# Normed activations and one feed-forward's gated rows at other byte positions in SBUF, an adaLN ring of two tiles, masks loaded as bytes

## The chip, the cores and the metric

The kernel runs on one core of a Trainium2 chip. The metric is the time of one execution in microseconds of device time; three runs of the kernel before gave 1816.92, 1817.19 and 1819.23 us, so a median of 1817.19 us. One more execution was recorded by the hardware profiler; it took 1819.16 us, and its span, from the first to the last instruction, is 1817.5 us.

## The reference

The model is a two-layer backbone over 256 latent tokens with 256 context tokens as a prefix, 1024 channels wide. Each layer is a feed-forward, a token mixer and a second feed-forward. Each of the three begins with an RMS norm that is scaled and shifted by vectors computed from a condition (adaLN), and its result is added back through a gate vector.

```python
def _swiglu(h, w1, w3, w2):
    return (jax.nn.silu(h @ w1) * (h @ w3)) @ w2
...
ml = _modulation(c, w_ada[l], b_ada[l])          # 9 vectors of 1024: silu(c) @ w_ada + b_ada
lat = lat + 0.5 * ml[2] * _swiglu(_modulate(lat, norm_ffn1_g[l], ml[0], ml[1]), *ffn1)
cx = cx + 0.5 * mc[2] * _swiglu(_modulate(cx, norm_ffn1_g[l], mc[0], mc[1]), *ffn1)
...                                              # token mixer: one input projection, spatial gating,
...                                              # a two-way gated recurrence, one output projection
lat = lat + 0.5 * ml[8] * _swiglu(_modulate(lat, norm_ffn2_g[l], ml[6], ml[7]), *ffn2)
```

The feed-forward is 2816 wide. Context tokens use the same weights; in the last layer only latent tokens go through the output projection and the second feed-forward.

## The kernel before

**Matmuls.** Every large product is made in three matmuls, because each float32 operand is split into a high and a low part (`mm3`, lines 285 to 288): high by high on L286, low activation by high weight on L287, high activation by low weight on L288 (where the weight is the moving operand the names are swapped). The weight block of 128x128 is the stationary operand. The activations are the moving one, in rows of 512 columns where latent and context tokens go together (`BOTH`), and of 256 columns where one of them goes alone (`LAT`, `CTXC`). The token-major units of the mixer (`tm_unit`, the i and v columns) turn this around: 128 tokens of the activations are stationary, and 256 weight columns move.

**Activations in SBUF.** `h_hi` and `h_lo` hold the normed activations: 8 blocks of 512 floats in each partition, one block for each 128 channels, the first 256 floats latent, the rest context. The norm writes them (`modulate`: ACT writes `h_hi`, DVE writes `h_lo`), and the up projections of the feed-forward and the mixer read them. `g_hi` and `g_lo` hold the gated rows of a feed-forward, 22 blocks, which the down projection reads. In the built program `h_hi` begins at byte 34304 of each partition and `h_lo` at 50688; both are multiples of 512. `g_hi` begins at byte 139072, and `g_lo` at 184128 (rows of 512) or at 161600 (the last feed-forward, rows of 256); all three are 320 bytes past a multiple of 512. A block is 2048 bytes (1024 in the last feed-forward's g, and each half of an h block is 1024), so every row of one buffer has its buffer's remainder. The split weights `whi` and `wlo` lie in four slots each, all at 64 bytes past a multiple of 512.

**Weights.** A weight piece is 512 rows by 256 columns (512 KB; some have half the rows). SP issues its DMA into one of 3 raw tiles, ACT copies it to `whi` (L187), DVE subtracts to get `wlo` (L191), and 4 such split pairs exist. A list made by `plan` sets the order of the pieces, and `pump` issues loads and splits ahead as far as the buffers allow.

**adaLN.** The modulation matrices are read in pieces `wada` of 128 x 512 floats (256 KB), 256 of them after the first few. They stand between the weight pieces in the plan, up to two at a time; they lie in a ring of `N_ADA` = 3 tiles. When the plan comes to one, `ada_sum` lets DVE multiply it by the condition and add it to `acc` (L247 for the first of eight, L249 for the others; twice for most pieces, once for the latent and once for the context condition). After eight pieces PE adds up the partitions (`ada_rows`, L258), in its own queue between two weight pieces. `pump` issues the next `wada` loads on SP right after a sum has been written down, each into the tile that was summed longest ago, so it waits for that sum on DVE.

**Masks.** The recurrence uses 7 masks of 128x128 bytes. They are loaded as float32 into `mf` at the start, and POOL casts them to bytes (L1019).

**Order.** Everything is issued in the order of the code; each engine works through its own queue. Around a feed-forward: 11 pairs of up columns (each four weight pieces), then four groups of down columns.

Of the kernel before, what the change touches and what calls it, by code (L numbers as in the profile page):

```python
# [10 lines left out]
F32 = mybir.dt.float32  # L11
F32R = mybir.dt.float32r
# [5 lines left out]
P = 128  # L18
# [3 lines left out]
T = SEQ + CTX  # L22
DEPTH = 2
GRID_W = 64
FF = 2816
KT = D // P
FT = FF // P
# [2 lines left out]
EPS = 1e-6  # L30
POS_THETA = 10000.0
NLEV = 7

COL = {"u": 0, "v": 512, "q": 1024, "f": 1536, "b": 2048, "i": 2560, "g": 3072}
LAT = (0, SEQ)
# [16 lines left out]
def level_masks():  # L52
    x = np.arange(P)[:, None] ^ np.arange(P)[None, :]
    m = np.stack([(x >> lev) == 1 for lev in range(NLEV)], axis=1)
    return np.ascontiguousarray(m.reshape(P, NLEV * P).astype(np.float32))

# [14 lines left out]
class Trunk:  # L73
    N_RAW = 3
    N_SPLIT = 4
    N_ADA = 3

    def __init__(self, tc, es, io):
        self.tc = tc
# [22 lines left out]
    def plan(self):  # L102
# [28 lines left out]
        for l in range(DEPTH):  # L131
            ws += ffn(l, 1, True) + mixer(l) + out(l) + ffn(l, 2, l + 1 < DEPTH)
# [23 lines left out]
    def pump(self):  # L156
        nc = self.nc
        moved = True
        while moved:
            moved = False  # L160
            if self.n_load >= 4 and self.a_load < min(len(self.adas), self.a_done + self.N_ADA):
                it = self.adas[self.a_load]
                _, l, j, half, k = it.key
                c0 = j * D + 512 * half
                it.raw = self.wp.tile([P, 512], F32, tag="ada", name="wada", bufs=self.N_ADA)
                nc.sync.dma_start(it.raw, self.io["w_ada"][l, k * P:(k + 1) * P, c0:c0 + 512])
# [117 lines left out]
    def mm3(self, ps, l_hi, l_lo, r_hi, r_lo, start, stop, swap=False):  # L284
        mm = self.nc.tensor.matmul
        mm(ps, lhsT=l_hi, rhs=r_hi, start=start, stop=False)  # L286
        mm(ps, lhsT=l_hi, rhs=r_lo, start=False, stop=False)  # L287
        mm(ps, lhsT=l_lo, rhs=r_hi, start=False, stop=stop)  # L288
# [113 lines left out]
    def ffn(self, l, n, both):  # L402
        nc = self.nc
        tc = self.tc
        w1, w3, w2 = (f"ffn{n}_w{i}" for i in (1, 3, 2))
        tokens = T if both else SEQ
        j0 = 0 if n == 1 else 6
        whole = BOTH if both else LAT
        with tc.tile_pool(name=f"g{l}{n}", bufs=1) as gp:
            g_hi = gp.tile([P, FT, tokens], F32R, tag="g_hi", name="g_hi")  # L410
            g_lo = gp.tile([P, FT, tokens], F32R, tag="g_lo", name="g_lo")

            silu = {}

            def gate(h, p, span, part):
                for j in range(2):
                    f = 2 * p + j
                    hi, lo = g_hi[:, f, span[0]:span[1]], g_lo[:, f, span[0]:span[1]]
                    ps = h[j][:, :span[1] - span[0]]
                    if part == 1:  # L420
                        silu[j] = self.sp.tile([P, 512], F32, tag="silu", name="silu", bufs=2)[:, :span[1] - span[0]]
                        nc.scalar.activation(silu[j], ps, AF.Silu)  # L422
                    else:
                        nc.vector.tensor_tensor(silu[j], silu[j], ps, op=ALU.mult)  # L424
                        self.split(hi, lo, silu[j])

            def up(p, span, its, keep=False):
                for part, w in ((1, w1), (3, w3)):
                    h = [self.bank(), self.bank()]
                    for i, k0 in enumerate((0, 4)):  # L430
                        it = its[part, k0] if its and not keep else self.take(w, l, k0, 256 * p)
                        self.fm(it, h, self.h_hi, self.h_lo, span, KT)
                        if keep:
                            its[part, k0] = it
                        else:
                            self.done(it)
                    gate(h, p, span, part)

            if self.begun:
                hs = self.begun  # L440
                self.begun = None
                for part, w in ((1, w1), (3, w3)):
                    it = self.take(w, l, 4, 0)
                    self.fm(it, hs[part], self.h_hi, self.h_lo, BOTH, KT)
                    self.done(it)
                    gate(hs[part], 0, whole, part)
            elif both:
                its = {0: None}
                up(0, LAT, its, keep=True)
                self.drain()  # L450
                up(0, CTXC, its)
            else:
                self.drain()
                up(0, LAT, None)
            for p in range(1, FF // 256):
                up(p, whole, None)

            def down(p, span):
                ps = [self.bank(), self.bank()]
                for k0 in range(0, FT, 4):  # L460
                    it = self.take(w2, l, k0, 256 * p)
                    self.fm(it, ps, g_hi, g_lo, span, FT)
                    self.done(it)
                self.update(l, j0 + 2, p, ps, span)

            for p in range(3):
                down(p, whole)
            down(3, LAT)
            if n == 1 or l + 1 < DEPTH:
                nl, nj = (l, 3) if n == 1 else (l + 1, 0)  # L470
                self.behind(self.norm(nl, nj, 0, NF[0]))
                if both:
                    down(3, CTXC)
                    self.drain()
                    self.behind(self.norm(nl, nj, 1, NF[1]))
# [18 lines left out]
    def hgrn(self, l, hp, mp, F, KB, q, V, ready, oT, ended):  # L494
# [12 lines left out]
        def keys(lev):  # L507
            b = 1 << lev
            ka = mp.tile([P, 2, nq], F32, tag="ks", name="ka", bufs=2 * two)
            for d in range(2):  # L510
                nc.scalar.activation(self.halves(ka, b)[d], self.halves(KB[:, d, :, :nq], b)[d], AF.Copy)
            return ka
# [22 lines left out]
        yield HQ[l]  # L535
        for lev in range(NLEV):
            b = 1 << lev
# [3 lines left out]
            for d in range(2):  # L541
                t = F[:, d, :, :n].rearrange("p h (n two) -> p h n two", two=2)
                kh = self.halves(KB[:, d], b)[d]
                tt(kh, kh, t[:, :, :, 1 - d, None].to_broadcast([P, 2, n // 2, b]), op=mult)
            if lev < NLEV - 1:
                ka = keys(lev + 1)
# [84 lines left out]
    def mixer(self, l):  # L631
# [7 lines left out]
        with tc.tile_pool(name=f"mix{l}", bufs=1) as mp:  # L639
# [196 lines left out]
            self.drain()  # L836
            self.behind(self.norm(l, 6, 1, NF[3]))


    def start(self):  # L840
        nc = self.nc
        io = self.io
        cp = self.cp
# [9 lines left out]
        for s in range(2):  # L853
            nc.vector.memset(self.sel[:, s, s:s + 1], 1.0)
        self.x = cp.tile([P, KT, T], F32, tag="x", name="x")
        self.h_hi = cp.tile([P, KT, T], F32R, tag="h_hi", name="h_hi")
        self.h_lo = cp.tile([P, KT, T], F32R, tag="h_lo", name="h_lo")
        self.ssq = cp.tile([P, T], F32, tag="ssq", name="ssq")
        self.mods = cp.tile([P, DEPTH * N_MOD, 2, KT], F32, tag="mods", name="mods")
        self.lb = cp.tile([P, 2, 2, 4], F32, tag="lb", name="lb")  # L860
        self.vec = [cp.tile([P, P], F32, tag=f"vec{l}", name="vec") for l in range(DEPTH)]
        self.masks = cp.tile([P, NLEV, P], U8, tag="masks", name="masks")
        with self.tc.tile_pool(name="start", bufs=1) as st:
            self.table(AF.Silu)
            cc = st.tile([16, P], F32, tag="cc", name="cc")
            pos = st.tile([P, 4 * 4 + 4 * GRID_W], F32, tag="pos", name="pos")
            mf = st.tile([P, NLEV * P], F32, tag="mf", name="mf")
            small = [(pos, io["pos"]), (cc[0:8, :], io["c"].rearrange("o (k p) -> (o k) p", p=P)),
                     (cc[8:16, :], io["c_ctx"].rearrange("(k p) -> k p", p=P))]
            rows = []  # L870
            for l, names in enumerate((("norm_ffn1_g", "norm_mix_g", "norm_ffn2_g", "norm_final_g"),
# [3 lines left out]
                at = 72  # L875
# [5 lines left out]
                    small.append((vr[at:at + r.shape[0], :], r))  # L881
                    at += r.shape[0]
                rows.append((vr, at))
            small.append((mf, io["masks"]))
            xs, raws = {}, {}

            def load(dst, src, after=1):
# [128 lines left out]
                self.fm(it, hs[part], self.h_hi, self.h_lo, BOTH, KT)  # L1016
                self.done(it)
            self.begun = hs
            nc.gpsimd.tensor_copy(self.masks.rearrange("p l t -> p (l t)"), mf)  # L1019

    def final(self):
        nc = self.nc
# [56 lines left out]
```

## Time and profile before

| | |
|---|---|
| median of three runs | 1817.19 us |
| profiled execution, its time | 1819.16 us |
| its span | 1817.5 us |
| mean granted TensorE clock | 0.995 |
| PE busy | 1785.7 us (98%) |
| DVE busy | 1125.8 us (62%) |
| ACT busy | 670.5 us (37%) |
| DMA, mean | 147 GB/s |

PE's busy time counts a matmul until its modelled end, and the next begins before that end. So a PE that is busy all the time can still run at different paces: the pace is the distance between the starts of two matmuls that follow each other, which the timeline gives.

### The profile page before, as it was taken

How to read it: one execution, taken by the hardware profiler on the slowest of the kernel's cores; microseconds unless marked ns; L12 is line 12 of the kernel's file. 1: busy time of each engine (PE TensorE's matmuls, PEld its weight loads, DVE VectorE, ACT ScalarE, POOL GpSimd, SP SyncE). 2: the span in 40 equal slices, each digit the busy share in tenths (PEclk: the TensorE clock that was granted, in tenths of full speed). 3: DMA queues.
4: the chain of work that ended last, by engine and by line, in shares of the span. 5: the costliest groups of instructions: out<-in, count | busy, mean ns of one | idle time of the engine just before them, and what ended most of it. 6: DMA issues, size and time to landing. Idle time of an engine off the chain costs nothing. (4 is left out here: it accounts for less than half of the span.)

```text
span 1817.5 us, 27049 instructions
## 1 busy us (share of the span) xinstructions
PE 1785.7 (98%) x10853; PEld 1547.7 (85%) x10853; DVE 1125.8 (62%) x1746; ACT 670.5 (37%) x1087; POOL 20.6 (1%) x27
## 2 busy tenths in 40 slices
PE   7999999999999999999999999999999999989998
PEld 5777778899898898777788897777788999979998
DVE  4766676675737666666666676545445767665554
ACT  3322222236444343222222242222222555544443
POOL 0000000000000000000000000000000000000000
PEclk9999999999999999999999999999999999989999
DMA  9555555554212124555454544544454532446653
GB/s 327 167 171 157 173 157 164 181 190 126 70 59 82 59 59 146 153 154 156 145 151 153 185 138 147 159 152 149 153 166 140 157 105 86 136 128 186 186 186 117
DMA packets 230645, 266.99 MB, mean 147 GB/s; under 512 B 10368, under 2 KB 192248, under 8 KB 230520
## 3 DMA queue, kind: packets, MB, share of 16 engines
q1 hardware_dynamic: 230520, 265.27, 47.2%
q8 instruction: 85, 1.39, 0.3%
q14 instruction: 40, 0.33, 0.1%
HBM read 264.18 MB, written 1.05 MB: 146 GB/s over the span
## 5 line engine op out<-in xcount | busy, mean ns | idle before, releaser
L286 PE MATMUL mm<-h_hi,whi 128*128 128x512 f32 (+1 forms) x2016 | 712.2, 353 | 4.9 <-ACT h_hi L383 3.0
L287 PE MATMUL mm<-h_lo,whi 128*128 128x512 f32 (+1 forms) x2016 | 705.2, 350 | 1.5 <-DVE h_lo L372 1.0
L288 PE MATMUL mm<-h_hi,wlo 128*128 128x512 f32 (+1 forms) x2016 | 702.6, 349 | 0.0
L191 DVE TENSOR_TENSOR wlo<-wraw,whi 128x1024 fp32r<-128x1024 f32 x362 | 430.7, 1195 | 371.8 <-ACT whi L187 367.8
L187 ACT ACTIVATE whi<-wraw 128x1024 fp32r<-128x1024 f32 x362 | 370.9, 1031 | 409.0 <-PE mm L287 288.0
L286 PEld LDWEIGHTS mm<-h_hi,whi 128*128 128x128 f32 x2016 | 381.0, 189 | 63.0 <-issue 4.0
L287 PEld LDWEIGHTS mm<-h_lo,whi 128*128 128x128 f32 x2016 | 382.7, 190 | 56.7 <-DVE h_lo L372 5.6
L288 PEld LDWEIGHTS mm<-h_hi,wlo 128*128 128x128 f32 x2016 | 380.7, 189 | 53.5
L286 PE MATMUL mm<-g_hi,whi 128*128 128x256 f32 (+1 forms) x836 | 282.1, 337 | 0.0
L288 PE MATMUL mm<-g_hi,wlo 128*128 128x256 f32 (+1 forms) x836 | 278.8, 334 | 0.0
L287 PE MATMUL mm<-g_lo,whi 128*128 128x256 f32 (+1 forms) x836 | 278.8, 333 | 0.0
L249 DVE SCALAR_TENSOR_TENSOR acc<-wada,cond,acc 128x512 f32<-128x512 f32 x392 | 274.0, 746 | 4.3 <-DMA wada<-in_w_ada_dram 3.4
L286 PEld LDWEIGHTS mm<-g_hi,whi 128*128 128x128 f32 x836 | 158.1, 189 | 18.3 <-issue 2.4
L288 PEld LDWEIGHTS mm<-g_hi,wlo 128*128 128x128 f32 x836 | 158.1, 189 | 16.0
L287 PEld LDWEIGHTS mm<-g_lo,whi 128*128 128x128 f32 x836 | 158.2, 189 | 15.2
L187 ACT ACTIVATE g_hi<-silu 128x512 fp32r<-128x512 f32 (+1 forms) x92 | 51.7, 562 | 182.9 <-DVE silu L424 181.0
L422 ACT ACTIVATE silu<-mm 128x512 f32<-128x512 f32 (+1 forms) x92 | 48.3, 528 | 139.7 <-PE mm L288 135.4
L191 DVE TENSOR_TENSOR g_lo<-silu,g_hi 128x512 fp32r<-128x512 f32 (+1 forms) x92 | 55.7, 605 | 57.9 <-ACT g_hi L187 57.9
L424 DVE TENSOR_TENSOR silu<-silu,mm 128x512 f32<-128x512 f32 (+1 forms) x92 | 54.9, 597 | 36.4 <-PE mm L288 36.4
L286 PE MATMUL mm<-whi,h_hi 128*128 128x256 f32 x224 | 64.3, 287 | 0.0
L287 PE MATMUL mm<-wlo,h_hi 128*128 128x256 f32 x224 | 62.6, 279 | 0.0
L288 PE MATMUL mm<-whi,h_lo 128*128 128x256 f32 x224 | 62.5, 279 | 0.0
(129 smaller groups left out, 1053.0 us busy)
## 6 DMA issues: line engine op xcount, KB each, us to landing
wraw<-in_ffn_w_dram SPq DMA_DIRECT2D x271, 512.0 KB, 4.3
wada<-in_w_ada_dram SPq DMA_DIRECT2D x256, 256.0 KB, 3.2
wraw<-in_w_in_dram SPq DMA_DIRECT2D x56, 512.0 KB, 3.6
a<-in_w_ada_dram SPq DMA_DIRECT2D x8, 1024.0 KB, 9.6
wraw<-in_w_out_dram SPq DMA_DIRECT2D x16, 512.0 KB, 3.9
wraw<-in_ffn_w_dram SPq DMA_DIRECT2D x19, 256.0 KB
x<-in_x_dram SPq DMA_DIRECT2D x2, 512.0 KB
ctx<-in_ctx_dram SPq DMA_DIRECT2D x2, 512.0 KB, 5.8
```

Of the source, the lines that this page charges most:

```text
L187: self.nc.scalar.activation(hi, src, AF.Copy)
L191: self.nc.vector.tensor_tensor(lo, src, hi.bitcast(F32), op=ALU.subtract)
L249: nc.vector.scalar_tensor_tensor(acc[:, s], raw, c, acc[:, s], op0=ALU.mult, op1=ALU.add)
L286: mm(ps, lhsT=l_hi, rhs=r_hi, start=start, stop=False)
L287: mm(ps, lhsT=l_hi, rhs=r_lo, start=False, stop=False)
L288: mm(ps, lhsT=l_lo, rhs=r_hi, start=False, stop=stop)
L422: nc.scalar.activation(silu[j], ps, AF.Silu)
L424: nc.vector.tensor_tensor(silu[j], silu[j], ps, op=ALU.mult)
```

## The change

Four things change.

1. `h_hi` and `h_lo` become longer buffers, `h_all`, and the rows have two homes in them, 80 floats (320 bytes) apart. `home(80)` is taken at the start: `h_hi` then begins at byte 34624 and `h_lo` at 52032, both 320 bytes past a multiple of 512. After the up projections of the last layer's first feed-forward, `home(0)` is taken: 34304 and 51712, both multiples of 512. From there on the last layer's mixer and its last feed-forward use it.
2. `g_hi` gets 128 or 48 unused floats ahead of it. With rows of 512 the gated rows lie where they lay (139072 and 184128). In the last feed-forward they lie at 138752 and 161280, both multiples of 512.
3. `N_ADA` goes from 3 to 2.
4. The masks are made as bytes and loaded straight into their place; `mf` and the cast go.

In the built program the split weights move by 1536 bytes, so they are still 64 bytes past a multiple of 512, and every other tile keeps its remainder by 512.

```diff
-    return np.ascontiguousarray(m.reshape(P, NLEV * P).astype(np.float32))
+    return np.ascontiguousarray(m.reshape(P, NLEV * P).astype(np.uint8))
...
-    N_ADA = 3
+    N_ADA = 2
...
-            g_hi = gp.tile([P, FT, tokens], F32R, tag="g_hi", name="g_hi")
+            lead = 128 if both else 48
+            g_hi = gp.tile([P, lead + FT * tokens], F32R, tag="g_hi", name="g_hi")[:, lead:]
+            g_hi = g_hi.rearrange("p (f t) -> p f t", t=tokens)
             g_lo = gp.tile([P, FT, tokens], F32R, tag="g_lo", name="g_lo")
...
                 up(p, whole, None)
+
+            if (l, n) == (DEPTH - 1, 1):
+                self.home(0)
...
+    def home(self, at):
+        self.h_hi, self.h_lo = (h[:, at:at + KT * T].rearrange("p (k t) -> p k t", t=T) for h in self.h_all)
...
-        self.h_hi = cp.tile([P, KT, T], F32R, tag="h_hi", name="h_hi")
-        self.h_lo = cp.tile([P, KT, T], F32R, tag="h_lo", name="h_lo")
+        self.h_all = [cp.tile([P, KT * T + n], F32R, tag=f"h_{w}", name=f"h_{w}")
+                      for w, n in (("hi", 256), ("lo", 128))]
+        self.home(SHIFT)
...
-            small.append((mf, io["masks"]))
+            small.append((self.masks.rearrange("p l t -> p (l t)"), io["masks"]))
...
-            nc.gpsimd.tensor_copy(self.masks.rearrange("p l t -> p (l t)"), mf)
```

The queues of PE, DVE and ACT hold the same instructions in the same order as before. SP's and POOL's differ in a few rows. SP's queue before, at the end of the start-up loads (`a` are the first adaLN pieces, `wraw` weight pieces):

```order
L891 DMA mf<-in_masks_dram 128x896
L174 DMA wraw<-in_ffn_w_dram 128x4x256 x2
L166 DMA wada<-in_w_ada_dram 128x512 x3
L174 DMA wraw<-in_ffn_w_dram 128x4x256 x5
L166 DMA wada<-in_w_ada_dram 128x512 x2
```

The same place now:

```order
L900 DMA masks<-in_masks_dram 128x896
L175 DMA wraw<-in_ffn_w_dram 128x4x256 x2
L167 DMA wada<-in_w_ada_dram 128x512 x2
L175 DMA wraw<-in_ffn_w_dram 128x4x256 x5
L167 DMA wada<-in_w_ada_dram 128x512 x2
```

Two pieces instead of three are loaded ahead, and each later `wada` load comes one piece later in the plan than it did; the last one moves behind one more weight piece.

POOL's queue before, around the cast (`r` is the reciprocal root of a norm):

```order
masks.py:199 AFFINE_SELECT ident<-ident 128x128
L331 TENSOR_TENSOR r<-ms,mhalf 128x2 x2
L1019 CAST masks<-mf 128x896
L331 TENSOR_TENSOR r<-ms,mhalf 128x2 x2
L331 TENSOR_TENSOR r<-ms,mhalf 128x4 x2
```

And now:

```order
masks.py:199 AFFINE_SELECT ident<-ident 128x128
L332 TENSOR_TENSOR r<-ms,mhalf 128x2 x4
L332 TENSOR_TENSOR r<-ms,mhalf 128x4 x2
L332 TENSOR_TENSOR r<-ms,mhalf 128x16
L332 TENSOR_TENSOR r<-ms,mhalf 128x4 x2
```

The cast is gone from POOL, and the rest stands as it stood.

## Rows read from the trace of the kernel before

**Rows 1.** The page's busy times: us, share of the span, instructions.
```profile
span 1817.5 us, 27049 instructions
PE 1785.7 (98%) x10853; PEld 1547.7 (85%) x10853; DVE 1125.8 (62%) x1746; ACT 670.5 (37%) x1087; POOL 20.6 (1%) x27
```

**Rows 2.** Windows: length; PE, PEld, DVE, ACT, POOL busy (instructions), PEclk, DMA share, GB/s.
```profile
556.30:654.70 98.40, 96.98 (x546) 83.58 (x545) 64.75 (x108) 41.12 (x77) 4.92 (x3) 1.00 0.21 65
702.80:932.00 229.20, 229.20 (x1064) 182.58 (x1064) 143.71 (x197) 66.17 (x87) 0.00 (x0) 1.00 0.52 156
932.00:1024.80 92.80, 92.80 (x449) 75.40 (x448) 58.01 (x85) 21.14 (x26) 0.00 (x0) 1.00 0.52 159
```

**Rows 3.** Groups of instructions, shapes kept apart: count | busy us, mean ns | idle before.
```profile
L286 PE MATMUL mm<-h_hi,whi 128*128 128x512 f32 x1184 | 475.6, 402 | 1.9 <-ACT h_hi L383 1.9
L286 PE MATMUL mm<-h_hi,whi 128*128 128x256 f32 x832 | 236.6, 284 | 3.0 <-ACT h_hi L187 1.9 <-ACT h_hi L383 1.1
L286 PE MATMUL mm<-g_hi,whi 128*128 128x512 f32 x396 | 156.2, 394 | 0.0
L286 PE MATMUL mm<-g_hi,whi 128*128 128x256 f32 x440 | 125.9, 286 | 0.0
```

**Rows 4.** PE's timeline (start, us, what), first and last of 119 512-column matmuls on h.
```profile
737.57 0.40 PE L287 MATMUL mm<-h_lo,whi 128*128 128x512 f32 x1
...
765.10 0.39 PE L288 MATMUL mm<-h_hi,wlo 128*128 128x512 f32 x1
```

**Rows 5.** The same, first and last of 107 512-column matmuls on g.
```profile
975.20 0.39 PE L287 MATMUL mm<-g_lo,whi 128*128 128x512 f32 x1
...
999.26 0.39 PE L288 MATMUL mm<-g_hi,wlo 128*128 128x512 f32 x1
```

**Rows 6.** The same, first and last of 143 256-column matmuls on g.
```profile
386.44 0.28 PE L287 MATMUL mm<-g_lo,whi 128*128 128x256 f32 x1
...
403.48 0.28 PE L288 MATMUL mm<-g_hi,wlo 128*128 128x256 f32 x1
```

**Rows 7.** First and last of 1038 256-column matmuls on h, last feed-forward.
```profile
1622.38 0.28 PE L286 MATMUL mm<-h_hi,whi 128*128 128x256 f32 x1
...
1744.51 0.28 PE L288 MATMUL mm<-h_hi,wlo 128*128 128x256 f32 x1
```

**Rows 8.** First and last of 108 256-column matmuls on h, output projection.
```profile
654.72 0.28 PE L286 MATMUL mm<-h_hi,whi 128*128 128x256 f32 x1
...
666.85 0.28 PE L288 MATMUL mm<-h_hi,wlo 128*128 128x256 f32 x1
```

**Rows 9.** First and last of 95 256-column matmuls with weights moving, h stationary.
```profile
514.08 0.28 PE L287 MATMUL mm<-wlo,h_hi 128*128 128x256 f32 x1
...
525.15 0.28 PE L288 MATMUL mm<-whi,h_lo 128*128 128x256 f32 x1
```

**Rows 10.** Tile wada: its DMA issues (ns min/median/max), and landing times.
```profile
L166 SPq DMA_DIRECT2D wada<-in_w_ada_dram x256: 327/328/2509, 30.2 to 1392.3; - x128
...
DMA to landing us min/median/max: 2.6/3.2/4.9
```

**Rows 11.** DVE's timeline, the first sums of one group of eight pieces.
```profile
140.01 0.88 DVE L247 TENSOR_SCALAR acc<-wada,cond 128x512 f32<-128x512 f32 x2
140.81 1.41 DVE L249 SCALAR_TENSOR_TENSOR acc<-wada,cond,acc 128x512 f32<-128x512 f32 x2
...
143.27 2.74 DVE L249 SCALAR_TENSOR_TENSOR acc<-wada,cond,acc 128x512 f32<-128x512 f32 x4
```

**Rows 12.** DVE's timeline, the last sums of another group.
```profile
272.46 2.73 DVE L249 SCALAR_TENSOR_TENSOR acc<-wada,cond,acc 128x512 f32<-128x512 f32 x4
```

**Rows 13.** PE's timeline, the partition sums (L258) of that group.
```profile
277.77 0.64 PE L258 MATMUL ada_ps<-acc,sel 128*32 128x128 f32 x16
```

**Rows 14.** Waits: who waited for whom, us in all, times, longest.
```profile
PE ada_ps L258 <- DVE acc L249: 0.6, 2, 0.3
```

**Rows 15.** The same, the start.
```profile
POOL masks L1019 <- DMA mf<-in_masks_dram: 18.5, 1, 18.5
```

More of the change, by code (lines that the diff above doesn't have):

```diff
@@ L32 @@
 NLEV = 7
+SHIFT = 80
 COL = {"u": 0, "v": 512, "q": 1024, "f": 1536, "b": 2048, "i": 2560, "g": 3072}
@@ L866, in start @@
             pos = st.tile([P, 4 * 4 + 4 * GRID_W], F32, tag="pos", name="pos")
-            mf = st.tile([P, NLEV * P], F32, tag="mf", name="mf")
             small = [(pos, io["pos"]), (cc[0:8, :], io["c"].rearrange("o (k p) -> (o k) p", p=P)),
```

## The prediction

> **What bounds the kernel now.** I read the busy times first: PE is busy for 1785.7 of 1817.5 us, and no other engine comes near [rows 1]. The windows say the same for single stages: in the up projections of a feed-forward (702.80 to 932.00) and in its down projections (932.00 to 1024.80) PE has no idle time at all, at a granted clock of 1.00, which is the 2.4 GHz level, while DVE has a third or more to spare [rows 2]. So in these stages only two things count: the pace at which PE goes from one matmul to the next, and whether something new makes PE wait.
>
> For the pace the reader is to look at starts. On h, 119 matmuls of 512 columns begin between 737.57 and 765.10: 118 steps of 233.3 ns [rows 4]. On g, 107 matmuls of the same shape begin between 975.20 and 999.26: 106 steps of 227.0 ns [rows 5]. Rows of 256 columns go the other way round: 120.0 ns a step on g [rows 6], and on h 117.8 [rows 7] or 113.4 [rows 8]; h keeps to one of these two until something interrupts it. The mean durations lean the same way, 402 against 394 and 284 against 286 ns [rows 3]. [...] What differs between h and g in both comparisons is where a row begins: h at a multiple of 512 bytes, g 320 bytes past one. So I take the position as the cause, by inference; no row shows one buffer at both.
>
> **Part by part.** *Rows of 512 on h.* The change puts them where g's are, by the remainder. There are 3 x 1184 = 3552 [rows 3]. Of these 96 come after `home(0)` (two units of the last mixer: 2 units x 2 pieces x 8 x 3), so 3456 move. At 6.3 ns each that is 21.8 us. The first few matmuls after an interruption have other steps in both kernels, so I take 20.5. Bounds: 0 if the position doesn't matter, 21.8.
>
> *Rows of 256 on h at the new home.* The passes with latent or context tokens alone before `home(0)`: the first up columns of two feed-forwards (2 x 192), the first two units of the first mixer (192) and half of its output projection (192), 768 in all. They go to g's 120.0, from 117.8 or 113.4: a loss of 768 x 2.2 = 1.7 to 768 x 6.6 = 5.1 us. Both paces occur; I take 3.4.
>
> *Rows of 256 on g in the last feed-forward.* 4 x 22 x 2 x 3 = 528 matmuls go from 320 to a multiple of 512. At 117.8 that gives back 1.2 us, at 113.4 it gives 3.5. I take 1.2, since the feed-forward ahead of them, at such a position, stays at 117.8 for 1038 matmuls. Those matmuls keep their remainder and cost nothing new.
>
> *h as the stationary operand.* In the first mixer 384 matmuls (i and v) load h from the new place while weights move from the old remainder. They now take 117.8 [rows 9]. By the nearest rows they end between 113.4 and 120.0: 1.7 us less to 0.9 more; I take 0, as the moving operand stays.
>
> *The ring of two.* The DMAs are the same in number, each a piece later. Before, one tile was always loaded ahead. Now the third piece of a run goes into the first one's tile. In the example the first sums end at 140.89; the load lands 3.2 us later by the median, and some 0.3 for the issue comes on top [rows 10, 11]. So the third piece's sums begin at 144.4 rather than at 143.27, 1.1 us late. Behind them on DVE stand the next weight split and the gate. Each of these has cover: a split is made some three weight pieces ahead of PE, and one piece is 24 steps of 233 ns, 5.6 us; and DVE has idle time in every group. What has little cover is PE's partition sum, which stands in PE's queue and needs the eighth piece: at 277.77 it comes 2.6 us after the last sum's end at 275.19 [rows 12, 13], and twice it has no slack at all and waits, 0.6 us in all [rows 14]. Behind it in PE's queue is the whole stream of matmuls. There are 32 such partition sums. If a group's sums are late by 1.1 us for two or three of its pairs and DVE's idle time takes back about as much as it does now, most stay inside the slack; I take 3 us in all. Bounds: 0, and 32 x 1.1 = 35 if nothing had cover. SP itself loses nothing: a weight load behind a `wada` load waits for a split that stands behind the same sums.
>
> *The masks.* The cast and its wait of 18.5 us are on POOL, which nothing waits for here [rows 15]. 448 KB of DMA at the start become 112 KB, behind the loads that the first matmuls need: 0, at best 1 us less.
>
> *The first mixer.* 480 of the 3456 matmuls are in it, 2.9 us of the gain. There the recurrence on DVE paces some of the work: PE has 1.4 us idle in 98.4 [rows 2]. I take back 0.5; at worst all 2.9.
>
> Sum: -20.5 + 3.4 - 1.2 + 0 + 3 + 0 + 0.5 = -14.8 us. The profiled execution took 1819.16 us (a span of 1817.5 and 1.7 around it), 2 us above the median of the runs. Against itself it would come to 1804.4; against the median of 1817.19 the forecast is 1802.4, so 1802 us.
>
> [...]
>
> **The rivals.** *One: only two thirds of the long rows gain.* In h's new home the high and the low part lie 1024 bytes apart by a remainder of 2048 (34624 and 52032); g's two parts have the same remainder. If this relation counts, the 1152 matmuls on `h_lo` stay at 233.3. They are worth 7 us, and the time is 1809. For it: nothing in the rows has this relation. Against it: on g, latent and context rows begin 1024 bytes apart and both go at 120.0.
>
> *Two: the position is not the cause.* Then what remains is the ring's 3 us and at most small change elsewhere: 1819 to 1820, within the measurement. For it: h and g are read in different stages. Against it: the turned sign, and that h keeps 233.3 whatever stage it is in.
>
> *Three, slower: the ring's loads land late.* With two weight loads and two `wada` loads asked for closely together the landing may go from 3.2 toward the longest seen, 4.9 us [rows 10]. Each pair of sums is then 4.9 + 0.35 - 2.38 = 2.9 us late, where 2.38 is what lies between the end of a sum and the next use of its tile (140.89 to 143.27); four pairs make up to 11 us for a group, beyond the slack of 2.6 and DVE's idle time. I put it at 3 us of PE wait for each of the 14 groups in the first feed-forward, whose plan asks for two at a time: 42 us at 4.9, where the time is 1799.4 + 42 = 1841. Between 3 us at 3.2 and 42 at 4.9 a straight line reaches 17.8, all that the other parts give, at a landing of about 3.9 us on average; from there it decides. Against it: the median of 256 loads is 3.2.
>
> **How the numbers follow.** Forecast, 1802 with its own range of 1795 to 1807: 0.70. Rival one, 1809: 0.09. Rival two, 1819: 0.13. Rival three, 1820 and more: 0.04. Better than forecast, with the last feed-forward's g at 113.4 or no ring cost: 0.04. The range of 1793 to 1813 holds forecast, rival one and a mild form of rival three. What a measurement here can tell from no change is about 0.2%, 3.6 us. Faster: 0.70 + 0.09 + 0.04 = 0.83. Same: rival two, less what goes to the slow side, 0.12. Slower: 0.05.
>
> **What would show it.** In the profile after, runs on h in the up projections should step at 227.0 ns, those of 256 columns there at 120.0, and the last down projections at 117.8. PE's waits for `acc` should be a few us, and DVE should now wait for `wada` by about 1 us at a time. If the steps on h stay at 233.3, the position is not it; if `h_lo` alone stays, rival one; if the wait of L258 for `acc` is 15 us or more, rival three.

## The result, and the profile after

The changed kernel takes 1795.47 us, the median of four runs (1794.83 to 1796.53); the kernel before took 1817.34 beside it (1816.92 to 1819.23). The ratio is 0.9878, with a 95% interval of 0.9861 to 0.9895, so 21.9 us are gone. The forecast was 14.8 us and 1802; 1795.47 lies at the lower edge of its own range, 1795 to 1807. The profiled execution took 1796.01 us, 23.15 less than the one of before.

PE's busy time in the page of the changed kernel, to be read beside [rows 1]:

```profile
span 1794.2 us, 27050 instructions
PE 1763.5 (98%) x10853; PEld 1544.1 (86%) x10853; DVE 1130.4 (63%) x1746; ACT 670.6 (37%) x1087; POOL 19.6 (1%) x26
```

PE is as busy as before, for 22.2 us less, with as many matmuls. The windows of an up and a down projection, in the columns of [rows 2]:

```profile
698.40:921.90 223.50, 223.50 (x1064) 182.30 (x1063) 144.69 (x197) 65.92 (x87) 0.00 (x0) 1.00 0.54 160
922.00:1014.70 92.70, 92.70 (x448) 75.37 (x448) 58.09 (x86) 21.15 (x26) 0.00 (x0) 1.00 0.52 159
```

The up projection is 5.7 us shorter at the same granted clock, the down projection as long as it was. Now the pace. These are rows of PE's timeline of the changed kernel, the first and the last matmul of undisturbed stretches: 512 columns on h (120 matmuls), 256 columns on h at the new home (108), weights moving over stationary h (95), 256 columns on h in the last feed-forward (1032), and on g there (528). (The line numbers are one higher than before: L287 to L289 are the three matmuls of L286 to L288.)

```profile
698.42 0.40 PE L287 MATMUL mm<-h_hi,whi 128*128 128x512 f32 x1
...
725.42 0.39 PE L289 MATMUL mm<-h_hi,wlo 128*128 128x512 f32 x1
...
649.36 0.28 PE L287 MATMUL mm<-h_hi,whi 128*128 128x256 f32 x1
...
662.19 0.28 PE L289 MATMUL mm<-h_hi,wlo 128*128 128x256 f32 x1
...
509.52 0.28 PE L288 MATMUL mm<-wlo,h_hi 128*128 128x256 f32 x1
...
520.79 0.29 PE L289 MATMUL mm<-whi,h_lo 128*128 128x256 f32 x1
...
1607.40 0.28 PE L287 MATMUL mm<-h_hi,whi 128*128 128x256 f32 x1
...
1724.26 0.28 PE L289 MATMUL mm<-h_hi,wlo 128*128 128x256 f32 x1
1724.38 0.28 PE L287 MATMUL mm<-g_hi,whi 128*128 128x256 f32 x1
...
1784.10 0.28 PE L289 MATMUL mm<-g_hi,wlo 128*128 128x256 f32 x1
```

Each pair gives a step, the difference of the starts over the number of steps: 226.9, 119.9, 119.9, 113.35 and 113.3 ns. Taken with the means over the whole of each group (steps of up to 245 ns for 512 columns and up to 127 for 256, so without the interruptions), the differences make up the gain:

| group | count | step before, ns | step after, ns | us | forecast |
|---|---|---|---|---|---|
| h, 512 columns, new home | 3456 | 233.4 | 227.4 | -20.6 | -20.5 |
| h, 256 columns, new home | 768 | 115.5 | 119.9 | +3.4 | +3.4 |
| h stationary, first mixer | 384 | 117.5 | 119.9 | +0.9 | 0 |
| g, 256 columns, last feed-forward | 528 | 120.0 | 113.3 | -3.5 | -1.2 |
| h, 256 columns, rest of the last mixer (384) and last up projections (1056) | 1440 | 117.35 | 113.74 | -5.2 | 0 |
| h, 256 columns, first units of the last mixer | 240 | 116.5 | 114.05 | -0.6 | 0 |

That is -25.6. The rest to -23.15 is +2.5: the first of these matmuls starts at 27.6 us instead of 26.7, the end after the last of them is 0.5 longer, and about 1 is spread over interruptions.

The waits of the changed kernel (who for whom, us in all, times, longest), to [rows 14], and the landing of `wada`, to [rows 10]:

```profile
PE ada_ps L259 <- DVE acc L250: 0.7, 2, 0.3
DVE acc L250 <- DMA wada<-in_w_ada_dram: 34.3, 50, 1.9
```

The second of these before:

```profile
DVE acc L249 <- DMA wada<-in_w_ada_dram: 3.4, 5, 0.8
```

The landing now:

```profile
DMA to landing us min/median/max: 2.5/2.9/4.8
```

DVE now waits for `wada` 50 times instead of 5, for up to 1.9 us. PE does not notice: its wait for `acc` is as it was.

### The profile page after: what moved, and what is told of

Same layout as the page of the kernel before. It is cut to its first block, busy times and chain, and to the rows that moved or that the text cites. A ratio compares the mean times of both kernels' runs of the same rounds, so it can differ in the third digit from the quotient of the medians.

```text
span 1794.2 us, 27050 instructions
## 1 busy us (share of the span) xinstructions
PE 1763.5 (98%) x10853; PEld 1544.1 (86%) x10853; DVE 1130.4 (63%) x1746; ACT 670.6 (37%) x1087; POOL 19.6 (1%) x26
## 5 line engine op out<-in xcount | busy, mean ns | idle before, releaser
L287 PE MATMUL mm<-h_hi,whi 128*128 128x512 f32 (+1 forms) x2016 | 705.5, 350 | 5.0 <-ACT h_hi L384 3.0
L288 PE MATMUL mm<-h_lo,whi 128*128 128x512 f32 (+1 forms) x2016 | 698.4, 346 | 1.3 <-DVE h_lo L373 1.0
L289 PE MATMUL mm<-h_hi,wlo 128*128 128x512 f32 (+1 forms) x2016 | 695.7, 345 | 0.0
L188 ACT ACTIVATE whi<-wraw 128x1024 fp32r<-128x1024 f32 x362 | 371.1, 1032 | 396.5 <-PE mm L288 274.3
L287 PEld LDWEIGHTS mm<-h_hi,whi 128*128 128x128 f32 x2016 | 382.1, 190 | 56.6 <-issue 4.0
L288 PEld LDWEIGHTS mm<-h_lo,whi 128*128 128x128 f32 x2016 | 382.0, 190 | 50.8 <-DVE h_lo L373 5.5
L289 PEld LDWEIGHTS mm<-h_hi,wlo 128*128 128x128 f32 x2016 | 381.9, 189 | 47.2
L250 DVE SCALAR_TENSOR_TENSOR acc<-wada,cond,acc 128x512 f32<-128x512 f32 x392 | 275.9, 748 | 36.4 <-DMA wada<-in_w_ada_dram 34.3
L287 PE MATMUL mm<-g_hi,whi 128*128 128x256 f32 (+1 forms) x836 | 280.7, 336 | 0.0
L289 PE MATMUL mm<-g_hi,wlo 128*128 128x256 f32 (+1 forms) x836 | 277.5, 332 | 0.0
L288 PE MATMUL mm<-g_lo,whi 128*128 128x256 f32 (+1 forms) x836 | 277.5, 332 | 0.0
L287 PEld LDWEIGHTS mm<-g_hi,whi 128*128 128x128 f32 x836 | 157.9, 189 | 18.4 <-issue 2.4
L289 PEld LDWEIGHTS mm<-g_hi,wlo 128*128 128x128 f32 x836 | 158.0, 189 | 15.7
L288 PEld LDWEIGHTS mm<-g_lo,whi 128*128 128x128 f32 x836 | 158.0, 189 | 15.2
L287 PE MATMUL mm<-whi,h_hi 128*128 128x256 f32 x224 | 64.8, 289 | 0.0
L288 PE MATMUL mm<-wlo,h_hi 128*128 128x256 f32 x224 | 63.0, 281 | 0.0
L289 PE MATMUL mm<-whi,h_lo 128*128 128x256 f32 x224 | 63.0, 281 | 0.0
```

Of the source, the lines that this page charges most:

```text
L188: self.nc.scalar.activation(hi, src, AF.Copy)
L250: nc.vector.scalar_tensor_tensor(acc[:, s], raw, c, acc[:, s], op0=ALU.mult, op1=ALU.add)
```

## The experiments

**The ring alone.** The kernel before with one number changed.

```diff
-    N_ADA = 3
+    N_ADA = 2
```

> The kernel before with the adaLN ring at two tiles and nothing else. If the ring costs next to nothing (the reading of the profile after, where PE waits 0.7 us for acc as before): 1817 to 1818 us, PE's wait for acc 1 us or less, DVE's wait for wada some 35 us. If the ring costs PE what the prediction put on it: 1820 us, with 3 us of PE wait for acc. The steps of the matmuls stay at 233.4 ns on h and 227 on g for 512 columns.

1816.87 us, the median of ten runs, against 1816.3 (ratio 0.9999, 0.9986 to 1.0012, so at most some 2.2 us more). Its waits:

```profile
DVE acc L249 <- DMA wada<-in_w_ada_dram: 30.0, 47, 2.0
PE ada_ps L258 <- DVE acc L249: 0.6, 2, 0.3
```

DVE waits 30 us in all, PE as little as with three tiles. The ring costs nothing that can be measured, and brings none of the gain: 512 columns on h stay at 233.4 ns. But h goes at 113.8 in the mean from the rest of the last mixer to the last up projections, where the first profile of before has 117.35, with h and the weights where they were.

**The weights moved, h not.** The rows of h keep the two homes of the changed kernel; a pad of 192 bytes behind the masks moves all tiles that follow, the weights among them; g moves as well.

```diff
-            lead = 128 if both else 48
+            lead = 0 if both else 48
...
         self.masks = cp.tile([P, NLEV, P], U8, tag="masks", name="masks")
+        cp.tile([P, 48], F32, tag="pad", name="pad")
```

The weights now begin 256 bytes past a multiple of 512, g in rows of 512 columns at a multiple of 512, where h had been slow; the last feed-forward's g at 192; h where it is in the changed kernel, at 320 and then at 0.

> The changed kernel with everything that lies behind the masks moved on, so that the split weights begin 256 bytes past a multiple of 512 instead of 64; h stays at its two homes, and the gated rows of 512 columns now lie at a multiple of 512, those of the last feed-forward 192 past one. Theory one, the position of the moving row alone counts: 512 columns on h 227.4 ns a step, on g 233.4; 256 columns in the last up projections stay at 113.5 to 117.8. Theory two, what counts is where the moving row begins against the weights (256 bytes apart goes at 227 and 120, 448 apart at 233 and 113 to 118): g at 512 columns stays at 227, the last up projections (256 apart) go to 120.0, the last g (448 apart) at 113.3 to 117.8, and h at 512 columns (64 apart) at a step that no run has shown.

1804.8 us, one execution. The timeline of this kernel, first and last matmul of stretches on h (120 matmuls of 512 columns), g (107) and the last h (1034 of 256 columns):

```profile
696.68 0.40 PE L287 MATMUL mm<-h_hi,whi 128*128 128x512 f32 x1
...
723.93 0.40 PE L289 MATMUL mm<-h_hi,wlo 128*128 128x512 f32 x1
...
934.05 0.40 PE L288 MATMUL mm<-g_lo,whi 128*128 128x512 f32 x1
...
958.09 0.39 PE L289 MATMUL mm<-g_hi,wlo 128*128 128x512 f32 x1
...
1609.13 0.28 PE L288 MATMUL mm<-h_lo,whi 128*128 128x256 f32 x1
...
1733.08 0.28 PE L289 MATMUL mm<-h_hi,wlo 128*128 128x256 f32 x1
```

h, which was not moved, steps at 229.0 ns instead of 226.9. g, at a multiple of 512, keeps 226.8. The last h, not moved either, goes from 113.35 to 120.0. So it is not where a row begins that sets the pace, but how far it begins from something that was moved: from the weights h is now 64 bytes on (it was 256), g 256 before them, the last h 256 before them. That it is the weights, and not another of the moved tiles, is shown only by the last experiment, which moves the weights piece by piece.

**The second home left out.** The changed kernel with h at 320 to the end, 256 bytes past the weights throughout.

```diff
-            if (l, n) == (DEPTH - 1, 1):
-                self.home(0)
```

> The changed kernel without home(0): h stays 320 bytes past a multiple of 512 to the end, so 256 bytes from the weights. Theory two (distance from the weights): the last up projections go to 120.0 ns a step, 1440 matmuls x 6.3 = 9 us more than in the changed kernel, the last mixer's 96 long rows from 233.2 to 227.4, its i and v units from 117.7 to 119.9; in all some 1804 us. If home(0) is not what makes those rows fast: 113.7 stays, and 1795 us.

1805.63 us, one execution. First and last of 1033 matmuls on the last h:

```profile
1610.04 0.28 PE L289 MATMUL mm<-h_hi,wlo 128*128 128x256 f32 x1
...
1733.88 0.28 PE L289 MATMUL mm<-h_hi,wlo 128*128 128x256 f32 x1
```

120.0 ns a step, as on g: the second home is worth 9.6 us beside the changed kernel's profile (1796.01), 8.9 of them from the 1440 matmuls of the table (119.95 against 113.74). At the slower of the two paces that the next run shows for these rows, 117.35 in the mean, it would be some 3.7 of these 8.9.

**The kernel before once more.** One empty line more (so the line numbers are one higher) and nothing else; a second profile.

> The kernel before, unchanged, recorded once more. It tells whether the pace of 256-column rows on h is fixed by the kernel. If it is fixed by the positions: 1438 of the matmuls in the last up projections at 117.4 ns in the mean again. If it is set anew in each execution by when PE was interrupted: some other mixture of 113.4 and 117.8, as far as 113.8 in the mean, 5 us less in that stage.

1818.68 us. First and last of 1029 matmuls on the last h:

```profile
1627.21 0.28 PE L287 MATMUL mm<-h_hi,whi 128*128 128x256 f32 x1
...
1743.73 0.28 PE L289 MATMUL mm<-h_hi,wlo 128*128 128x256 f32 x1
```

113.35 ns a step, where [rows 7] give 117.8. Nothing else in its groups differs by more than 0.2 ns. So this pair of paces is not the program's: one execution has the one, another the other. (The time is hardly less than in the first profile because the first matmul on h starts 2.5 us later and the first stage takes 1.1 more.)

The two profiles part in the output projection ahead of these rows. In both, PE waits 1.66 us there for h and soon runs at a granted clock of 0.50, the 1.2 GHz level. These are windows of that spell in the first profile and in the second, in the columns of [rows 2]:

```profile
1595.90:1598.20 2.30, 2.30 (x11) 2.27 (x11) 0.64 (x2) 0.42 (x1) 0.00 (x0) 0.50 0.45 155
1600.00:1603.10 3.10, 3.10 (x16) 3.10 (x16) 1.48 (x4) 1.78 (x3) 0.00 (x0) 0.50 0.02 8
```

The first and last matmul of the stretches behind it, 105 in the first profile and 95 in the second:

```profile
1598.42 0.28 PE L286 MATMUL mm<-h_hi,whi 128*128 128x256 f32 x1
...
1610.67 0.28 PE L288 MATMUL mm<-h_hi,wlo 128*128 128x256 f32 x1
...
1603.34 0.28 PE L288 MATMUL mm<-h_lo,whi 128*128 128x256 f32 x1
...
1614.01 0.28 PE L289 MATMUL mm<-h_hi,wlo 128*128 128x256 f32 x1
```

Out of it the first goes on at 117.8 ns a step, the second at 113.5, and each has its pace again in the last up projections. So the pace can change where PE was interrupted; what decides between the two is not shown.

**Sixteen homes.** Four kernels, each with four homes for h, one for each stage (the first feed-forward; the first mixer and the second feed-forward; the third; the last mixer and feed-forward); the weights stay at 64 past a multiple of 512. They differ in one line.

```diff
+HOMES = (16, 32, 48, 64)
...
-            if (l, n) == (DEPTH - 1, 1):
-                self.home(0)
+            if (l, n) != (DEPTH - 1, 2):
+                self.home(HOMES[2 * l + n])
...
-        self.home(SHIFT)
+        self.home(HOMES[0])
```

The others have (96, 112, 128, 8), (20, 24, 28, 56) and (76, 72, 60, 68) floats.

> The changed kernel with a home of its own for each layer's half: 64 bytes past a multiple of 512 up to the first feed-forward, 128 for the first mixer and its second feed-forward, 192 for the last layer's first feed-forward, 256 for the last mixer and feed-forward. Theory one, a row that begins on a multiple of 512 is the slow one and any other goes like g: 227.4 ns a step at 512 columns in all three, and 120.0 at 256 columns in the last up projections. Theory two, the step follows the distance from the weights: different steps in the three stages, 233 near 64 bytes, and 227 only toward 256 bytes of distance.

> As the run before it, with homes 384, 448 and 512 bytes past (the last is a multiple of 512 again, at another place than the old one), and 32 bytes past for the last mixer and feed-forward. Theory one: 227.4 ns at 384 and 448, 233.4 at 512, and 120.0 at 256 columns in the last up projections. Theory two: steps that change from stage to stage with the distance from the weights, and at 512 the old 233.4 as well.

> The changed kernel with finer distances between the moving rows of h and the weights: 16 bytes up to the first feed-forward, 32 for the first mixer and its feed-forward, 48 for the last layer's first feed-forward, and 160 for the last mixer and feed-forward. If the step goes by the distance modulo 256 and changes smoothly between the tried points: 512 columns from 227.6 (0) up to 229.1 (64), so 228.0, 228.4, 228.7; 256 columns at 160 between 118.6 and 113.4. If it changes by lines of 64 bytes: 227.6, and 118.6.

> The same with distances of 240, 224, 176 and 208 bytes (modulo 256). Smooth: 512 columns at 240 about 229, at 224 about 231, at 176 233.3; 256 columns at 208 between 113.4 and 115. By lines of 64 bytes: 233.4 at 240, 224 and 208 for 512 columns, 232.9 at 176, and 113.4 or 117.8 for 256 columns at 208.

1800.4, 1817.19, 1815.17 and 1822.05 us, one execution each. In the first of them, the first and last of 120 matmuls of 512 columns 128 bytes from the weights:

```profile
1072.82 0.40 PE L287 MATMUL mm<-h_hi,whi 128*128 128x512 f32 x1
...
1100.59 0.40 PE L289 MATMUL mm<-h_hi,wlo 128*128 128x512 f32 x1
```

233.4 ns; the mean of that stage is 232.9. All of these stages and the kernels above give this table, in mean ns a step of each group of rows; "distance" is the start of the moving row less the start of the stationary weights, by remainder of 256 bytes.

| distance | 512 columns | 256 columns |
|---|---|---|
| 0 | 227.2 to 227.9 | 119.7 to 120.0 |
| 16 | 231.7 | |
| 32 | 233.3 | 117.0 to 117.4 |
| 48 | 232.9 | 118.3 |
| 64 | 229.0 to 229.7 | 115.8 to 117.8 |
| 128 | 232.5 to 232.9 | 118.6 to 119.1 |
| 160 | 234.2 | 117.5 to 118.0 |
| 176 | 233.3 | 119.3 |
| 192 | 233.1 to 233.4 | 113.3 or 117.8, also mixed |
| 208 | 233.5 | 119.0 to 119.2 |
| 224 | 233.0 to 233.3 | 118.3 to 118.5 |
| 240 | 233.4 | |

The period is 256: 64 and 320 give the same for 512 columns (229.0 to 229.7 and 229.1), and so do 0 and 256. Within the period it is neither a smooth curve nor a step at each 64 bytes: at 16 bytes 231.7, over two thirds of the loss. For 512 columns only 0 is good, and 64 keeps some two thirds of the gain; for 256 columns 0 is the worst and 192 the best.

The means of 256 columns can mix two paces, and not at 192 alone. These are the first and last of 85 matmuls on h in the first mixer of the kernel of *The weights moved, h not*, 64 bytes from the weights: 113.3 ns a step, where the other rows at 64 go at 117.8.

```profile
425.87 0.28 PE L289 MATMUL mm<-h_hi,wlo 128*128 128x256 f32 x1
...
435.39 0.28 PE L289 MATMUL mm<-h_hi,wlo 128*128 128x256 f32 x1
```

Of what was expected, theory one fails in the first two kernels, since rows off a multiple of 512 go at 229 and 233 too. Theory two holds there, but its figures were put in the wrong place: a home at 64 bytes is no distance from the weights, and goes at 227.7. In the last two kernels neither the smooth curve nor the step by lines holds throughout. Below 64 bytes both fail for 512 columns (231.7 to 233.3), from 176 on the step by lines is about right for them, and the 119.0 of 256 columns at 208 fits neither.

**Each pass at its best distance.** The changed kernel with the weights laid by the pass that uses them: 0, 64, 128 or 192 bytes further on, so that 512 columns stand at 0 and 256 columns at 192, also where the weights move.

```diff
-                it.hi = self.wp.tile([P, 4, 256], F32R, tag="hi", name="whi", bufs=self.N_SPLIT)
-                it.lo = self.wp.tile([P, 4, 256], F32R, tag="lo", name="wlo", bufs=self.N_SPLIT)
+                at = self.place(it.key)
+                pair = self.wp.tile([P, 2 * 1024 + 64], F32R, tag="pair", name="whl", bufs=self.N_SPLIT)
+                it.hi, it.lo = (pair[:, a:a + 1024].rearrange("p (k c) -> p k c", c=256) for a in (at, at + 1024))
...
-            lead = 128 if both else 48
+            lead = 0 if both else 48
...
-                      for w, n in (("hi", 256), ("lo", 128))]
+                      for w, n in (("hi", 128), ("lo", 128))]
```

`place` gives 16 floats for a piece that is used by 256 columns alone, 48 or 32 for i and v, 48 for two units of the last mixer, 0 for the rest. The two other edits keep h, g and the weights of place 0 at their remainders of 256.

> The changed kernel with the split weights laid 0, 64, 128 or 192 bytes further on, by the pass that uses the piece, so that the moving row stands 0 bytes (mod 256) from its weights in every pass of 512 columns and 192 bytes in every pass of 256; the whole output is computed. By the distance, with the paces of the runs before: 768 h rows of 256 columns 119.9 to 113.5 (4.9 us), 792 g rows of the three wide feed-forwards 119.9 to 113.5 (5.0), 384 'w' steps of layer 0 119.9 to 113.5 (2.4), 288 of layer 1 117.8 to 113.5 (1.2), 96 h rows of 512 in the last mixer 233.2 to 227.5 (0.5): 14.0 in all, so 1781.5 us. If this execution falls into the other of the two paces that stood at 192 bytes in the runs before (117.6 instead of 113.5), these rows gain a third of it and the last feed-forward's up rows lose: about 1791 to 1797. If only the 512-column rows go by the distance and the 256-column rows by something that this layout does not set: 1795, as the changed kernel.

> The changed kernel once more, for a comparison on one chip: 1795.5 us. If the up rows of the last feed-forward (113.74 ns in its profile, 117.35 in that of before, same distance) have a pace that is set anew in each execution, 1440 of them by 3.6 ns spread the single times by up to 5 us, and the profile shows either 113.7 or 117.4; if the pace belongs to the kernel, it shows 113.7 again.

On one chip the new version takes 1790.54 us (1788.36 to 1792.13, four runs), the changed kernel 1798.78 (1794.48 to 1802.83, six) and the kernel before 1816.59; the ratios to before are 0.9855 (0.9839 to 0.9872) and 0.9896 (0.9878 to 0.9914). Its slowest run is faster than the fastest of the changed kernel: this is the better kernel, by 8 us between the medians. 14.0 were expected at one pace and hardly any gain at the other. The timeline shows why it lies between; first and last on g in 256 columns (143 matmuls), h in 256 columns (108), moving weights (95):

```profile
382.01 0.28 PE L306 MATMUL mm<-g_lo,whl 128*128 128x256 f32 x1
...
398.74 0.28 PE L307 MATMUL mm<-g_hi,whl 128*128 128x256 f32 x1
...
646.02 0.28 PE L305 MATMUL mm<-h_hi,whl 128*128 128x256 f32 x1
...
658.62 0.28 PE L307 MATMUL mm<-h_hi,whl 128*128 128x256 f32 x1
...
507.64 0.28 PE L306 MATMUL mm<-whl,h_hi 128*128 128x256 f32 x1
...
518.31 0.28 PE L307 MATMUL mm<-whl,h_lo 128*128 128x256 f32 x1
```

117.8, 117.8 and 113.5 ns, all at distance 192, in one execution. Both paces occur, and a stretch keeps the one it has. By the means of the groups the edits gave 768 x 3.8 + 792 x 2.8 + 384 x 4.7 + 288 x 1.4 + 96 x 5.2 ns = 7.8 us; the two profiles (1796.29 and 1788.36) differ by 7.9. In the last of these groups, the long rows of the last mixer, only the weights were moved, and 233.2 became 228.0.

The single runs of the changed kernel beside it fall into two heaps of three, 1794.5 to 1796.3 and 1801.3 to 1802.8. Its profile is of the lower one and shows 113.74 for the last 1440 rows of 256 columns on h, as the first did. If the upper heap is that of 117.35 there, as in the first profile of before, and of 117.8 in the last g, as in the second of the sixteen-homes kernels, it should be 1440 x 3.6 + 528 x 4.5 ns = 7.6 us higher; about 7 were measured. The kernel before has heaps too: eight runs from 1814.9 to 1817.3 and three from 1819.6 to 1821.4. The means are 4.2 apart, where its rows on h would give 5.2. That fits, but no profile of an upper run of the changed kernel was taken.

## Why the prediction was right, and where it was not

*What bounds it.* Right: PE has no idle time in the windows of the projections, before or after, and the gain is in the steps between starts.

*Rows of 512 on h.* Right in size: -20.6 against -20.5. `h_lo` goes with `h_hi`, so rival one falls; rival two, that nothing depends on the layout, falls too. For it stood that h and g are read in different stages; but before the change h stepped at 233.2 ns in the first mixer and at 233.4 in the up projections, with DMA at 65 and at 156 GB/s [rows 2]. The Trainium skill's page "TensorE: Matmul & The Clock Gate", section "Back-to-back issue gap", gives 518 cycles (about 216 ns) as the gap of an isolated matmul of 512 columns and about 131 ns as the spacing in a stream with weight loads, neither by the layout. The trace does not agree: the runs here show from 227 to 234 ns, by the layout. The cause was given too simply. I took the position of the row, by its remainder of 512 bytes. The runs show the distance of the row from the stationary weights, by a remainder of 256. The weights stood still in this change, so both say the same of it; *The weights moved, h not* is where they part.

*Rows of 256 on h.* Right, +3.4, with both paces of before mixed as assumed.

*g of the last feed-forward.* The other bound came true: -3.5 instead of -1.2. I took 117.8 because the rows ahead of it were at 117.8 in the profile of before. The place does not fix that pace: with these rows 192 from the weights most profiles have 113.3 or 113.4, the second of the sixteen-homes kernels has 117.8. So it may have been chance which bound came.

*The last up projections.* "Those matmuls keep their remainder and cost nothing new": the change does nothing to them, yet 5.2 us of the difference between the two profiles are theirs and the last mixer's just ahead of them. The second profile of before has 113.75 there as well. So these 5.2 us, and 0.6 in the first units of the last mixer where *The ring alone* has 114.6 ns with h and the weights at the old places, are no gain of the change; that 21.9 us were measured is in part luck. Without them the two profiles differ by some 17.4 us, with the 2.5 of start, end and interruptions charged to the change; by the steps alone it is 19.8. In the later comparison, with six runs and eleven, the medians differ by 17.8, but they mix the heaps: half of the changed kernel's runs are in its upper one, three of eleven of the kernel before. Heap against heap the means differ by 21.1 (lower) and 18.5 (upper).

*h as the stationary operand.* Taken at 0, it came out at its upper bound, +0.9: the distance counts here too, where the weights are the moving operand and h the stationary one.

*The ring.* The step that failed: 3 us were taken, 0 measured, by itself. The chain was right up to DVE, which waits for `wada` 50 times; but 34.3 us over 50 waits is 0.7 us each, less than the 1.1 worked out, and the loads land after 2.9 us rather than 3.2. That the slack of 2.6 us before a partition sum holds it is likely, but was not measured in the changed kernel; what is shown is that PE's wait for `acc` did not grow, 0.6 and 0.7 us. Rival three would have needed 15 us of it.

*The masks and the first mixer.* Nothing can be seen of either: POOL's cast is gone, and the first mixer's interruptions grew by a few tenths at most.

In sum, by the terms: the ring 3, the last g 2.3, the take-back 0.5 too pessimistic, the stationary h 0.9 and the 2.5 of start, end and interruptions not counted; that would have made 17.2. Of the remaining 6.0, 5.8 are the pace of one execution against another's.

## What to carry to other kernels

In a kernel whose PE is never idle, read the step between the starts of matmuls for each pair of operands, and when two stages of one shape differ, compare where both operands begin, not the moving one alone. Here the placement of buffers was worth some 26 us (1816.6 to 1790.5) with the same matmuls; the ring, taken alone, gave nothing. Before a difference of a few us is credited to a change, profile the unchanged kernel twice: a step may belong to the execution.

## What was not expected of the hardware

- The step of a matmul on split float32 (moving and stationary operand in SBUF) depends on the distance between the two operands by a remainder of 256 bytes: 512 columns 227 ns at 0, 229 at 64, 232 to 234 at the other distances tried, already 231.7 at 16; 256 columns 120.0 at 0, 113.3 or 117.8 at 192. Why it does is not shown.
- At distance 192 rows of 256 columns have two paces, 113.4 and 117.8. A stretch of a thousand matmuls keeps one, the same program shows the one in one execution and the other in the next, and both can stand in one execution. At 64 both occur as well. Two profiles of the kernel before took different paces behind an interruption, at which the granted clock had fallen to 0.50 in both. What selects it was not found.
- The start differs between executions too: the first matmul on h began at 26.7 and at 29.2 us in two profiles of the kernel before.
